# A two-layer decoder step on one core: three projections moved to the end of local attention, norms as background steps, an odd layer that begins on two chunks

## The chip, the core and the metric

The kernel runs on one core of a Trainium2 chip. The core has a matrix engine (TensorE, PE in the profile), VectorE (DVE), ScalarE (ACT), GpSimd (POOL) and a queue processor (SyncE, SP) that issues most DMAs; ScalarE issues the others. Each engine works through its own list of instructions in order and waits for the others by semaphores. The metric is the device time of one launch in microseconds (us).

## The reference

One inference step of a decoder trunk with two layers, for a prompt of 1024 tokens and 8 sample tokens with cached state. All is float32. Cut to what the change touches:

```python
for layer in range(2):
    h = rms_norm(x, norm_pre[layer])                  # x: 1024 + 8 tokens, 1024 channels
    mkv = memory_kv(mem, mem_norm[layer], w_mem_kv[layer])      # 256 memory tokens
    if layer == 0:   # even: gated delta rule | local attention | memory attention
        parts = [dilated_group(q[g], k[g], v[g], window, dil)   # 3 groups x 4 heads
                 for g, (window, dil) in enumerate(((128, 1), (512, 4), (2048, 16)))]
        o_b = combine_dilations(parts) * silu(gate_b)  # merged by softmax denominators
        o_m = memory_attend(q_m, mkv) * silu(gate_m)   # 4 heads of 128
        mix = concat(o_a * silu(z_a), o_b, o_m)        # 12 blocks of 128 channels
    else:            # odd: RG-LRU (8 blocks) | memory attention (4 heads)
        mix = concat(rg_lru(conv(xb)) * silu(gate), o_m * silu(gate_m))
    x = x + rms_norm(mix @ w_out[layer], norm_post[layer])
```

## The kernel before

Channels lie on the 128 partitions, tokens along the free axis, in three chunks of 352, 336 and 344 tokens (0, 1 and 2; the 8 sample tokens end chunk 2). A projection (`proj`) loads one 128-column block of weights as eight 128x128 tiles and makes, for each chunk, 24 matmuls: each tile is split into a rounded part and its remainder (`load_w`: ScalarE rounds, GpSimd or, for the output weights, VectorE subtracts), the activations likewise, and three of the four products are added in PSUM (`mm3`). So a projection is 72 matmuls.

The program is written in this order, and a scheduler then lays each engine's list; what has high priority goes first, the rest about as written.

1. Memory keys and values, the first norm, and the gated delta rule (`even_gdn`). In its last part four heads run one after the other in a chain of eight small steps each (`chain`: matmuls that go to VectorE and back, at L897, L900, L905 and L907). Projections are put beside it as cover: memory heads 0 to 2, and 11 results that are needed later and are parked in DRAM (`swa_ahead`, the dictionary `ahead`).
2. Local attention (`even_swa`): 36 query, key and value projections (4 heads x 3 window groups x 3), five of them parked ones. Beside them run two lanes of background work: `group` (scores, softmax, products of one head and group) and `combine` (the three groups of a head merged by factors that go through DRAM and come back broadcast, `sfb`). A lane is a generator; `tick`, called after each chunk of a projection, lets each lane do its next piece.
3. Output layer (`out_layer`): 8 output blocks x 12 mix blocks; first chunks 0 and 1 (mix blocks held in SBUF as `mah` and `mal`), then chunk 2. The norms (`chain_a`, `chain_b`, made of `tok_rstd` and `chan_rstd`: columns of sums on PE (`c`), an inverse root of twelve small VectorE steps (`x`, `y`, `t`), a diagonal `d` and a matmul `b` that spreads it) turn the result into the next layer's input `h1`. Tiles of the norm after the output are named `po0` and the chunk, of the next layer's pre-norm `pr` and the chunk.
4. The memory keys and values of layer 1 (`mem_kv(1)`, weights `mk1`, `mv1`), then the odd layer (`odd`: `query` makes `wq1`, `conv` makes `wx`), then its own output layer.

At the end of stage 2, before the change, memory head 3's query and gate come back from DRAM, all lanes are drained, memory head 3 attends (`ms`, `mt`, `mo`), and only then the combine of local head 3 starts (`slt` is its first matmul). The blocks of the mix are used in the order 0 to 3, 8 to 10, 4, 5, 6, 11, 7: memory head 3 is block 11, local head 3 is block 7.

## Time and profile before

| | us |
|---|---|
| median of 3 runs | 1944.48 (1942.31 to 1946.13) |
| the profiled execution | 1943.99 |
| its span, first to last instruction | 1942.2 |
| PE busy | 1789.0 (92%) |
| VectorE busy | 1081.1 (56%) |
| ScalarE busy | 716.3 (37%) |
| GpSimd busy | 540.2 (28%) |

The granted clock of PE is 0.949 of full speed on average. A busy share says how long an engine had work in it; matmuls are pipelined, so a busy PE at a low granted clock, or one with gaps just under the length of a record, may do half the work of a full one. "Idle before <- X" is the time an engine stood still before an instruction, and what ended it.

### The profile page before, as it was taken

The numbers are of one execution on the slowest core, as the hardware profiler recorded it, in microseconds if no ns is written. First come the engines' busy times: TensorE is split into PE (matmuls) and PEld (weight loads), VectorE is DVE, ScalarE is ACT, GpSimd is POOL, SyncE is SP. The second block draws the span as 40 slices with busy tenths as digits, with TensorE's granted clock in tenths as the row PEclk, the third lists the DMA queues.
The fourth block names the chain that finished last, engine by engine and source line by source line (L and its number), as shares of the span: only waits on it lengthen the run. The fifth ranks groups of instructions, "written<-read, shape, count | busy, mean of one in ns | idle before, by whom it ended". The sixth has DMA issues, their size and how long they took to land.

```text
span 1942.2 us, 29187 instructions
## 1 busy us (share of the span) xinstructions
PE 1789.0 (92%) x11341; PEld 1729.4 (89%) x11341; DVE 1081.1 (56%) x2302; ACT 716.3 (37%) x1610; POOL 540.2 (28%) x367
## 2 busy tenths in 40 slices
PE   6999999898999899999999976977899999989996
PEld 6799988798999899999999856967799999988996
DVE  7878759446633313525325556558655747667555
ACT  5355533123222243433333432324333434436432
POOL 3422224222211113232533202123532424330201
PEclk9999998898999999999999987978899999999998
DMA  8436455633425534645655424356733332223453
GB/s 288 177 130 217 153 173 190 213 114 116 177 102 197 188 120 148 239 143 180 221 184 193 140 67 151 114 154 223 257 133 143 130 111 96 78 71 125 144 193 135
DMA packets 160986, 307.30 MB, mean 158 GB/s; under 512 B 25104, under 2 KB 120528, under 8 KB 158928
## 3 DMA queue, kind: packets, MB, share of 16 engines
q1 hardware_dynamic: 67168, 222.99, 33.1%
q10 hardware_dynamic: 93680, 82.45, 13.0%
q8 instruction: 89, 1.46, 0.3%
q14 instruction: 49, 0.40, 0.1%
HBM read 254.58 MB, written 138.81 MB: 203 GB/s over the span
## 4 chain that ended last, share of the span: by engine, by line
PE 73%; DVE 15%; DMA 5%; ACT 3%; issue 2%; ACTq 1%; POOL 1%; SPq 0%; DVEq 0%; POOLq 0%
PE ss L992 1%; PE so L1025 1%; PE mo L373 1%; DVE tm L734 1%; PE ms L352 1%; PE gz L857 1%; PE gt L862 1%; DMA mf<-mixd 1%; PE st L1015 1%; PE mt L370 1%; DVE lacc L1270 1%; DVE got L934 1%; DVE xi L736 1%; DMA o_memv<-vf 1%; PE svp L977 1%
## 5 line engine op out<-in xcount | busy, mean ns | idle before, releaser
L994 DVE CUSTOM_DVE_ANT_0 spr<-ss,cs 128x128 f32<-128x128 f32 (+1 forms) x96 | 31.9, 348 | 84.9 <-PE ss L992 84.5
L1001 ACT ACTIVATE spr<-spr,snm 128x128 f32<-128x128 f32 (+1 forms) x96 | 42.2, 441 | 40.0 <-DVE snm L996 39.8
L628 DVE SCALAR_TENSOR_TENSOR acc<-pre,vec,acc 128x1024 f32<-128x1024 f32 x36 | 49.2, 1366 | 13.4 <-ACT acc L626 13.2
L1369 DVE TENSOR_TENSOR ya<-ya,ysq 128x352 f32<-128x352 f32 (+2 forms) x42 | 27.0, 645 | 37.4 <-ACT ysq L1368 37.4
L992 PE MATMUL ss<-sw,sw 128*128 128x128 f32 (+1 forms) x192 | 43.5, 330 | 4.1 <-DVE sml L994 2.8
L358 ACT ACTIVATE pm<-ms,nm 128x256 f32<-128x256 f32 x64 | 29.7, 472 | 47.0 <-DVE nm L356 34.7
L1427 POOL TENSOR_TENSOR y<-y,xr 128x352 f32<-128x352 f32 (+2 forms) x24 | 22.4, 936 | 84.9 <-DVE y L1426 84.3
L1384 POOL COPY mg<-mixs 128x8 f32<-128x8 f32 x24 | 7.7, 319 | 125.9 <-DVE wo01al L154 25.2
L372 DVE COPY mpt<-mt 128x512 f32<-128x512 f32 x32 | 22.0, 688 | 36.4 <-PE mt L370 36.3
L373 PE MATMUL mo<-mpt,vt 128*128 128x512 f32 x64 | 34.9, 628 | 4.9 <-DVE gnr L120 3.2
L978 DVE COPY svt<-svp 128x512 f32<-128x512 f32 x24 | 15.5, 684 | 41.6 <-PE svp L977 36.1
L1025 PE MATMUL so<-spt,svt 128*128 128x128 f32 x280 | 38.3, 275 | 0.2 <-ACT spt L1019 0.2
L1228 DVE SCALAR_TENSOR_TENSOR lacc<-lpre,vec,lacc 128x1024 f32<-128x1024 f32 x24 | 37.4, 1560 | 0.2
L1025 PEld LDWEIGHTS so<-spt,svt 128*128 128x128 f32 x280 | 36.3, 191 | 0.5 <-ACT spt L1019 0.5
L992 PEld LDWEIGHTS ss<-sw,sw 128*128 128x128 f32 x192 | 31.6, 195 | 5.3 <-DVE sml L994 3.3
L1225 DVE TENSOR_SCALAR lacc<-lpre,vec 128x1024 f32<-128x1024 f32 x8 | 19.4, 2419 | 23.7 <-ACT lpre L1220 23.7
L734 DVE TENSOR_TENSOR tm<-bl,xi 128x1 f32<-128x1 f32 (+30 forms) x31 | 28.5, 920 | 2.5 <-DMA bl<-aqd 2.0
L898 DVE TENSOR_TENSOR guu<-guu,gsc 128x128 f32<-128x128 f32 x28 | 8.0, 284 | 38.5 <-PE gsc L897 38.4
L162 PE MATMUL wo00p<-mah,wo00ah 128*128 128x352 f32 (+1 forms) x24 | 8.6, 401 | 22.5 <-ACT mah L1334 22.5
L370 PEld LDWEIGHTS mt<-cs,pm 128*128 128x128 f32 x128 | 17.5, 147 | 13.2 <-issue 8.0
L1019 ACT COPY spt<-st 128x384 f32<-128x384 f32 (+2 forms) x48 | 22.5, 475 | 17.4 <-PE st L1015 15.4
L352 PE MATMUL ms<-kt,qm 128*128 128x256 f32 x112 | 28.7, 387 | 0.0
(2149 smaller groups left out, 7344.4 us busy)
## 6 DMA issues: line engine op xcount, KB each, us to landing
o_sw3s<-cache_swa SPq DMA_DIRECT2D x64, 1023.5 KB
o_sw2s<-cache_swa SPq DMA_DIRECT2D x16, 1022.0 KB
gaq<-aqd ACTq DMA_DIRECT2D x20, 512.0 KB
mf<-mixd SPq DMA_DIRECT2D x19, 344.0 KB
sfb<-fd SPq DMA_DIRECT2D x12, 512.0 KB
aqd<-aq ACTq DMA_DIRECT2D x4, 1024.0 KB
o_sw3p<-sw SPq DMA_DIRECT2D x8, 512.0 KB
mixd<-lgt ACTq DMA_DIRECT2D x8, 512.0 KB
```

Source lines behind the costliest of these rows:

```text
L352: T.matmul(ps[:, b * 256:(b + 1) * 256], q[:, (b0 + b) * P:(b0 + b + 1) * P], kt[:, h, :], start=True, stop=True)
L358: S.activation(pr[:, b2 * 2 + b, :], ps[:, b * 256:(b + 1) * 256], AF.Exp, bias=nm[:, b0 + b:b0 + b + 1], scale=SC, accum_out=lt[:, b0 + b ...
L370: T.transpose(pt[:, b * P:(b + 1) * P], pr[:, b, kb * P:(kb + 1) * P], ident)
L373: T.matmul(po, vt[:, kb, h, :], st, start=kb == 0, stop=kb == 1)
L628: V.scalar_tensor_tensor(acc, pre[:, j:j + 1024], vc("gconv", ti * 4 + j), acc, ALU.mult, ALU.add)
L734: V.tensor_tensor(t3, bl[:, 0:i, i][:, None, :].broadcast_to([P, i, i]), xi[:, 0:i, 0:i].rearrange("p j c -> p c j"), ALU.mult)
L992: T.matmul(po, q[:, bb * P:(bb + 1) * P], k[:, k0:k0 + w], start=True, stop=True)
L994: V.tensor_tensor_reduce(pr[:, bb, :w], po, mask, 1.0, NEG, ALU.add, ALU.max, accum_out=ml[:, 0, g, bb:bb + 1])
L1001: S.activation(pr[:, bb, :w], pr[:, bb, :w], AF.Exp, bias=nm[:, bb:bb + 1], scale=SC, accum_out=ml[:, 1, g, bb:bb + 1])
L1025: T.matmul(po[:, (bb % 4) * P:(bb % 4 + 1) * P], vt[:, kb, :], pt[:, o:o + P], start=st, stop=sp_)
L1228: V.scalar_tensor_tensor(acc[:, :1024], pre[:, j:j + 1024], vc("lconv", ti * 4 + j), acc[:, :1024], ALU.mult, ALU.add)
L1369: V.tensor_tensor(acc[:, :n], acc[:, :n], sq[:, :n], ALU.add)
```

## The change

Local attention. The parked results are now 10. Memory head 3's query and gate and local head 3's gate are no longer among them, and two projections of local head 1, group 0 (query and key) are new. The three left out are projected in `even_swa` itself, after the last value projection and before the lanes are drained. The combine of head 3 is started by its lane like the others, memory head 3's attention calls `tick` four times, and the mix order ends with 7, 11.

Output layer. `tok_rstd` and `chan_rstd` become generators that give way after the squares and after the diagonal. In layer 0 the norms of chunks 0, 1 and 2 are lanes; before, they were issued at high priority. In layer 1 the norms are taken as lanes too for chunks 0 and 1.

Odd layer. The first query and the first convolution input are projected for chunks 0 and 1 first, then both for chunk 2. Their tiles move to a pool of their own, opened earlier. Two pools shrink to make room: `hf` from three buffers to two, `ysq` of layer 0 from two to one.

```diff
@@ even_gdn
-                    for key in ((), (), (("q3",), ("g3",), (1,)), ((0, 0, 1), (0, 0, 2), (2,), (3,)))[h]:
+                    for key in ((), (), ((1,), (2,), (1, 0, 0)), ((0, 0, 1), (0, 0, 2), (1, 0, 1)))[h]:
@@ mem_attend
+                if ticks:
+                    tick()
@@ even_swa
-                    if g == 2 and h < 3:
-                        lanes["group"].append([then("combine", combine(h, ml, nums, lambda acc, h=h: put(h, acc))), 0])
+                    if g == 2:
+                        done = (lambda acc, h=h: put(h, acc)) if h < 3 else (lambda acc: last.update(acc=acc))
+                        if h == 3:
+                            gt = sp.tile([P, 1024], F32, name="sg3", tag="sg")
+                        job = combine(h, ml, nums, done, gt if h == 3 else None)
+                        lanes["group"].append([then("combine", job), 0])
...
+            swa_gate(3, x, sp, gt)
+            qm = sp.tile([P, 1024], F32, name="qm03", tag="qkv", bufs=5)
+            mem_query(0, 3, x, I["we"][59], qm)
+            gm = mem_gate(sp, 0, 3, x, I["we"][63], "qkv", 5)
             sh0.close()
...
-            drain_lanes("cached", "group", "combine")
-            mem_attend(sp, 0, 3, qm, gm, gm, tags=("spr", "spt"))
-            mix_put(xa, order[-2], gm)
-            start("combine", combine(3, ml, nums, lambda acc: last.update(acc=acc)))
+            drain_lanes("cached", "group")
+            mem_attend(sp, 0, 3, qm, gm, gm, tags=("spr", "spt"), ticks=True)
...
@@ out_layer
-                    with tc.high_priority(offset=HP):
-                        if l:
-                            chain(m, xr[m])
-                        elif m == 0:
-                            chain_a(0, xr[0])
-                        else:
-                            chain_a(1, xr[1])
-                            chain_b(0)
-                            chain_b(1)
+                    start(f"norm{m}", chain(m, xr[m]))
...
-            with tc.high_priority(offset=HP):
-                chain(2, xr[2])
+            drain_lanes("norm0", "norm1")
             if l == 0:
+                start("norm2", chain(2, xr[2]))
+                tick()
                 mem_kv(1, mem_reload(pb), np_)
+                drain_lanes("norm2")
@@ odd
-                if n < 3:
+                if n == 0:
+                    q0 = query(0, (0, 1))
+                    begun = {0: conv_in(0, 0, (0, 1))}
+                    q0()
+                elif n < 3:
                     query(n)
-                conv(n, 0)
+                conv(n, 0, begun.get(0))
```

The first place in the order is PE's list at the end of local attention. `ws322p` is the last value projection, `wb3p`, `wq03p` and `wg03p` are the gate of local head 3 and the query and gate of memory head 3, `svp`, `ss` belong to the last window group, `slt` begins the last combine, and `wo00p` is the first output block. Before:

```order
L164 MATMUL ws322p_10523<-h0h_140,ws322l_10455 128x344
L977 MATMUL svp_10588<-cs,sw_10452 128x128 x4
...
L992 MATMUL ss_10604<-sw_10305,sw_10168 128x128
L162 MATMUL wo00p_10887<-mah_10559,wo00ah_10761 128x352
...
L370 MATMUL mt_10748<-cs,pm_10719 128x128 x4
L373 MATMUL mo_10739<-mpt_10753,vt_279 128x512
L1032 MATMUL slt_10778<-cs,sml_9307 48x128
L162 MATMUL wo00p_10887<-mah_10581,wo00ah_10768 128x352
```

Now:

```order
L164 MATMUL ws322p_10234<-h0h_140,ws322l_10165 128x344
L162 MATMUL wb3p_10278<-h0h_94,wb3h_10272 128x352
...
L162 MATMUL wq03p_10432<-h0h_94,wq03h_10426 128x352
...
L162 MATMUL wg03p_10556<-h0h_94,wg03h_10550 128x352
...
L1044 MATMUL slt_10592<-cs,sml_9032 48x128
L162 MATMUL wg03p_10598<-h0h_110,wg03h_10550 128x336
...
L164 MATMUL wg03p_10634<-h0h_140,wg03l_10551 128x344
L366 MATMUL ms_10694<-kt_278,qm_10424 128x256 x2
L162 MATMUL wo00p_10883<-mah_10667,wo00ah_10794 128x352
...
L389 MATMUL mo_10775<-mpt_10781,vt_279 128x512
L162 MATMUL wo00p_10883<-mah_10681,wo00ah_10801 128x352
```

Three projections stand where the output blocks stood, and `slt` has moved from behind memory head 3's attention to the middle of the last of them.

The second place is VectorE's list there. `mal` is the remainder of a mix block, `nm` the row maxima of memory head 3, `smm` and `sf` the factors of the combine, `snum` its large products, `sg` and `gm` or `smg` the gates. Before:

```order
L374 TENSOR_TENSOR smg_10584<-mo_10739,smg_10584 128x512
L1335 TENSOR_TENSOR mal_10582<-smg_10584,mah_10581 128x688
L1052 TENSOR_TENSOR smm_10804<-al_10788 8x128
...
L1063 SCALAR_TENSOR_TENSOR sf_10805<-sf_10805,smm_10804 8x384
L1078 TENSOR_TENSOR snum_9929<-snum_9929,sfb_10827 128x1024
L1080 TENSOR_TENSOR snum_10339<-snum_10339,sfb_10829 128x256x4
...
L1087 TENSOR_TENSOR snum_9929<-snum_9929,sg_10825 128x1024
L1335 TENSOR_TENSOR mal_10574<-snum_9929,mah_10573 128x688
```

Now:

```order
L368 TENSOR_REDUCE nm_10691<-ms_10694 128x2
L1361 TENSOR_TENSOR mal_10668<-mf_10807,mah_10667 128x688
...
L1064 TENSOR_TENSOR smm_10701<-al_10626 8x128
...
L1075 SCALAR_TENSOR_TENSOR sf_10702<-sf_10702,smm_10701 8x384
L1361 TENSOR_TENSOR mal_10678<-mf_10844,mah_10677 128x688
...
L1091 TENSOR_TENSOR snum_9644<-snum_9644,sfb_10725 128x1024
L154 TENSOR_TENSOR wo01al_11002<-wo01af_11000,wo01ah_11001 128x768
...
L1100 TENSOR_TENSOR snum_9644<-snum_9644,sg_10270 128x1024
L1361 TENSOR_TENSOR mal_10682<-snum_9644,mah_10681 128x688
L390 TENSOR_TENSOR gm_10548<-mo_10775,gm_10548 128x512
L1361 TENSOR_TENSOR mal_10690<-gm_10548,mah_10689 128x688
```

The combine stood alone behind memory head 3's attention; now its steps alternate with that attention and with the mix blocks.

The third place is PE's list at the end of the last delta-rule chain, where `gsc` are the chain's steps, `ws011p` is the projection beside it and `gf` begins the finish. Before:

```order
L897 MATMUL gsc_5709<-gS_5701,gWT_5592 128x128
L163 MATMUL ws011p_6280<-h0l_135,ws011h_6222 128x344
...
L164 MATMUL ws011p_6280<-h0h_140,ws011l_6223 128x344
L900 MATMUL gsc_5709<-guu_5591,gkd_5626 128x128
L905 MATMUL gsc_5709<-guu_5591,gaq_5510 128x128
L907 MATMUL gsc_5709<-gS_5701,gaq_5511 128x128
L935 MATMUL gf_6309<-cs,got_5635 128x128 x4
```

Now:

```order
L164 MATMUL ws011p_6179<-h0h_140,ws011l_6122 128x344
L912 MATMUL gsc_5698<-guu_5591,gkd_5626 128x128
L917 MATMUL gsc_5698<-guu_5591,gaq_5510 128x128
L919 MATMUL gsc_5698<-gS_5690,gaq_5511 128x128
L909 MATMUL gsc_5709<-gS_5701,gWT_5592 128x128
L912 MATMUL gsc_5709<-guu_5591,gkd_5626 128x128
L917 MATMUL gsc_5709<-guu_5591,gaq_5510 128x128
L919 MATMUL gsc_5709<-gS_5701,gaq_5511 128x128
L947 MATMUL gf_6208<-cs,got_5635 128x128 x4
```

The chain now ends with three matmul pairs and no projection between them, where before the last half step had 11 matmuls of a projection in it.

## Rows read from the trace of the kernel before

**Rows 1.** Seven stretches: engines' busy time, PE clock, DMA share; first line names the columns.

```profile
core 0: us, PE busy (x) PEld busy (x) DVE busy (x) ACT busy (x) POOL busy (x), PEclk, DMA share, GB/s
...
652.00:1102.50 450.50, 446.89 (x2961) 441.13 (x2961) 168.53 (x412) 163.84 (x388) 136.04 (x75) 0.99 0.52 176
1102.50:1144.50 42.00, 36.31 (x206) 32.08 (x204) 27.06 (x56) 18.54 (x47) 3.92 (x4) 0.92 0.40 130
1144.50:1184.40 39.90, 13.23 (x40) 9.29 (x40) 21.52 (x32) 5.93 (x16) 0.36 (x2) 0.62 0.19 59
...
1263.00:1296.20 33.20, 19.57 (x76) 16.84 (x75) 14.08 (x32) 4.88 (x10) 8.64 (x5) 0.65 0.46 139
1296.20:1337.10 40.90, 40.47 (x265) 39.43 (x264) 35.24 (x87) 23.39 (x50) 8.31 (x9) 0.99 0.75 254
1337.10:1391.00 53.90, 35.46 (x218) 32.88 (x217) 46.93 (x74) 22.65 (x42) 35.00 (x22) 0.76 0.58 200
1391.00:1411.50 20.50, 19.25 (x102) 18.70 (x101) 9.35 (x28) 4.68 (x10) 6.21 (x5) 0.80 0.63 234
```

**Rows 2.** PE timeline: start, duration, operation, idle before and its releaser.

```profile
1102.35 0.32 PE L164 MATMUL ws322p<-h0h,ws322l 128*128 128x344 f32 x1
...
1154.15 0.42 PE L1032 MATMUL slt<-cs,sml 128*48 128x128 f32 x1
...
1180.69 0.94 PE L162 MATMUL wo00p<-mah,wo00ah 128*128 128x352 f32 x2 [20.95 <-ACT mah L1334]
...
1184.37 0.32 PE L162 MATMUL wo02p<-mah,wo02ah 128*128 128x352 f32 x1
...
1195.64 0.32 PE L162 MATMUL wo03p<-mah,wo03ah 128*128 128x352 f32 x1
```

**Rows 3.** VectorE by form, 1102.5 to 1184.4: count, busy us, mean ns, idle before.

```profile
L1335 DVE TENSOR_TENSOR mal<-mf,mah 128x688 fp32r<-128x688 f32 x10 | 8.6, 870 | 2.3 <-ACT mah L1334 2.3
...
L421 DVE TENSOR_REDUCE sc2op<-sc2v 128x128 f32<-128x1152 f32 x3 | 6.6, 2194 | 0.0
```

**Rows 4.** VectorE timeline, last combine.

```profile
1169.63 1.23 DVE L1078 TENSOR_TENSOR snum<-snum,sfb 128x1024 f32<-128x1024 f32 x1 [5.60 <-DMA sfb<-fd]
```

**Rows 5.** PE timeline, end of the last delta-rule chain.

```profile
643.46 0.39 PE L897 MATMUL gsc<-gS,gWT 128*128 128x128 f32 x2
...
645.42 0.38 PE L900 MATMUL gsc<-guu,gkd 128*128 128x128 f32 x2
646.25 0.49 PE L905 MATMUL gsc<-guu,gaq 128*128 128x128 f32 x2 [0.44 <-DVE gS L902]
...
652.01 1.97 PE L935 MATMUL gf<-cs,got 128*128 128x128 f32 x8 [5.04 <-DVE got L934]
```

**Rows 6.** PE timeline, the last window group's steps.

```profile
1103.49 1.09 PE L977 MATMUL svp<-cs,sw 128*128 128x128 f32 x8 [0.82 <-ACT sw L495]
...
1106.48 0.49 PE L992 MATMUL ss<-sw,sw 128*128 128x128 f32 x2 [1.35 <-DVE svt L978]
...
1110.12 0.79 PE L992 MATMUL ss<-sw,sw 128*128 128x128 f32 x2 [1.66 <-DVE sml L994]
...
1118.10 0.71 PE L992 MATMUL ss<-sw,sw 128*128 128x128 f32 x4 [1.12 <-DVE sml L994]
```

**Rows 7.** VectorE timeline, norm of chunk 1.

```profile
1347.35 2.35 DVE L118 TENSOR_TENSOR pr1t<-pr1y 128x3 f32<-128x3 f32 x1
...
1350.12 0.15 DVE L119 SCALAR_TENSOR_TENSOR pr1t<-pr1t,pr1x 128x3 f32<-128x3 f32 x1
```

**Rows 8.** GpSimd timeline, same moment.

```profile
1347.29 2.40 POOL L154 TENSOR_TENSOR mk12l<-mk12f,mk12h 128x1024 fp32r<-128x1024 f32 x1 [0.32 <-ACT mk12h L152]
```

**Rows 9.** PE timeline, norms and the odd layer's start.

```profile
1355.83 0.90 PE L193 MATMUL pr1b<-pr1d,cs 128*128 128x336 f32 x1 [6.30 <-DVE pr1d L192]
...
1404.37 0.74 PE L193 MATMUL pr2b<-pr2d,cs 128*128 128x344 f32 x2
...
1406.37 0.42 PE L162 MATMUL wq10p<-h1h,wq10h 128*128 128x344 f32 x1 [1.25 <-ACT h1h L212]
```

More of the change, by code (lines that the diff above doesn't have):

```diff
@@ L167, in proj, with run, at_once @@
         w = load_w(aps, name)
-        for ci in chunks:
-            c0 = CH[ci][0]
-            n = x[ci][0][0].shape[1]
-            ps = banks["p"].tile([P, 512], F32, name=f"{name}p{ci}", tag="pp")
-            mm3(ps[:, :n], w, x[ci], pace)
-            drain(ci, c0, n, ps[:, :n])
-            tick()
+        def run(chunks):
+            for ci in chunks:
+                c0 = CH[ci][0]
+                n = x[ci][0][0].shape[1]
+                ps = banks["p"].tile([P, 512], F32, name=f"{name}p{ci}", tag="pp")
+                mm3(ps[:, :n], w, x[ci], pace)
+                drain(ci, c0, n, ps[:, :n])
+                tick()
+        run(chunks)
+        return lambda: run([c for c in (0, 1, 2) if c not in chunks])
+    def at_once(steps):
+        while True:
+            try:
+                next(steps)
+            except StopIteration as e:
+                return e.value
     def tok_rstd(pool, sqs, n, scale, name, pt=None):
@@ L276, in mem_norm @@
         rs = pool.tile([P, 256], F32, name="mrs0")
-        V.tensor_copy(rs, chan_rstd(pool, [xm[:, k, :] for k in range(8)], 256, "mr"))
+        V.tensor_copy(rs, at_once(chan_rstd(pool, [xm[:, k, :] for k in range(8)], 256, "mr")))
         nc.scalar.dma_start(out=rsd, in_=rs)
@@ L340, in silu_drain, with mem_attend @@
         return f
-    def mem_attend(pool, l, h, q, gate, mix, tags=("pm", "mpt")):
+    def mem_attend(pool, l, h, q, gate, mix, tags=("pm", "mpt"), ticks=False):
         kt, vt = kts[l], vts[l]
@@ L1067, in combine @@
                 fbs = []
-                gt = sp.tile([P, 1024], F32, name=f"sg{h}", tag="sg")
-                nc.sync.dma_start(out=gt, in_=ahead[h,])
+                if gt is None:
+                    gt = sp.tile([P, 1024], F32, name=f"sg{h}", tag="sg")
+                    nc.sync.dma_start(out=gt, in_=ahead[h,])
                 for g in range(3):
@@ L1135, in even_swa @@
             drain_lanes("combine")
-            mix_put(xa, order[-1], last["acc"])
-            nc.scalar.dma_start(out=mixd[0][:, 7, CA:], in_=last["acc"][:, CA:])
+            for k, t in ((7, last["acc"]), (11, gm)):
+                mix_put(xa, k, t)
+                nc.scalar.dma_start(out=mixd[0][:, k, CA:], in_=t[:, CA:])
             return xa, w0
@@ L1220, in d, with conv @@
                     S.copy(pre[:, 3 + c0:3 + c0 + w], ps)
-                proj([I["wo"][ti]], x, f"wx{ti}", d)
+                return pre, proj([I["wo"][ti]], x, f"wx{ti}", d, chunks)
+            def conv(n, m, begun=None):
+                ti = n * 2 + m
+                pre, rest = begun or conv_in(n, m)
+                rest()
                 G.tensor_copy(cs4[:, 3, ti], pre[:, 1027:1035])
@@ L1512, in body @@
     order = [0, 1, 2, 3, 4, 5, 8, 9, 10, 11, 6, 7]
-    xa, w0 = odd(h1, sh1, sxa, order)
+    xa, w0 = odd(h1, sh1, eo, sxa, order)
     assert not bulk
```

64 lines of the change are left out of this document (28 added, 36 removed).

## The prediction

> **What bounds the kernel now.** I read the busy shares first: PE is busy for 1789.0 of the 1942.2 us of the span, and no other engine comes near. So a gain can only come from time in which PE stands still or runs slowly, and the windows by stage say where that is [rows 1]. In local attention up to its last value projection (652.0 to 1102.5) PE is busy for 446.89 of 450.5 us at a granted clock of 0.99; there is nothing to gain there, and its length is the number of its projections. Behind it, from the last `ws322p` at 1102.35 to the first `wo02p` at 1184.37 [rows 2], PE is busy for 36.31 + 13.23 = 49.5 of 81.9 us, at 0.92 and then 0.62. The timeline says why: PE waits 20.95 us for the mix block `mah` before it can go on with `wo00p` [rows 2], that is, for the last combine, of which VectorE and a DMA broadcast (a wait of 5.60 us) are the chain [rows 4]. The second weak stretch is the output layer: 1263.0 to 1296.2 at a clock of 0.65, and 1337.1 to 1391.0 with 35.46 of 53.9 us at 0.76 [rows 1]. The third is the end of the last delta-rule chain, where PE waits 5.04 us for `got` [rows 5].
>
> The unit of the sum is a projection. `wo02p` takes 72 matmuls of the same widths from 1184.37 to 1195.64 [rows 2], and the next block begins right behind it: 11.27 us, in a full stretch.
>
> **The change part by part.** The count of projections stays the same. One goes from the delta rule, two from the middle of local attention, and three come to its end.
>
> *Delta rule.* One projection fewer is -11.27 us if PE is the bound there. But the last chain then ends with one more bare half step: from L897 to L900 it is 645.42 - 643.46 = 1.96 us, from L900 to L905 0.83 us, together 2.79 [rows 5], of which PE's own two records fill about 0.7 that it had to do anyhow. So +2.1, and -9.2. Bounds: -11.3 (the bare steps cost nothing) and 0 (the chain with its waits was the bound, and the projection lay free beside it). I take a value near the first, since before the change the projection ran up to one step from the chain's end, with no wait listed before the matmul at 645.42 that follows it [rows 5], which is what a full PE looks like.
>
> *Local attention, middle.* Two projections fewer, loaded instead: -22.5 us. Their loads are 512 KB each like those of the parked blocks, at a DMA share of 0.52 [rows 1], and far ahead of their use; at nothing. 29 projections now cover the window groups' steps instead of 31. Uncovered, one group waits 1.35 + 1.66 + 1.12 = 4.1 us [rows 6] (the last group is what shows it). For eleven groups, with 2 in 31 of the cover gone, that is 11 x 4.1 x 2/31 = 2.9 us. So -19.6; bounds -22.5 and, if the cover breaks everywhere, rival D.
>
> *The tail, last `ws322p` to first `wo02p`.* Before 81.9 us [rows 2]. Now three projections, 33.8 us, stand first, with the last group's steps between them; those of its matmuls that are listed take 1.09 + 0.49 + 0.79 + 0.71 = 3.1 us [rows 6], and I put the group at 5.5. So 39.3 us to the end of `wg03p`. What is late then is VectorE. It has 27.06 + 21.52 = 48.6 us of work in the old tail [rows 1]. Of that the three reductions `sc2op` (6.6 us [rows 3]) and the group's own steps (5, an estimate by the same share) now lie under the projections; 37 us are left: 12 remainders `mal` at 0.87 us [rows 3], the factors and products of the combine, memory head 3's maxima and gates. PE has less to do there. The 5.60 us of the broadcast [rows 4] now lie beside memory head 3 and the `mal` steps, since `slt` starts inside the last projection; the 20.95 us go with it. I add 4 us for the first drain and for the last rows of matmuls, which follow the last `mal`: 39.3 + 41 = 80.3, or -1.6. Below, PE's own work bounds it: 36.31 x 0.92 + 13.23 x 0.62 = 41.6 us at full clock [rows 1], + 33.8 = 75.4, or -6.5. Above, if the broadcast's wait stays and mix loads come late behind weights on SP's queue (another 3): +8. So two thirds of the gain of 32 us are there because the tail takes in three projections and gets no longer.
>
> *Norms as background steps.* The squares, roots and applications are the same instructions. What moves is their place: in the second pass the weight subtractions now go ahead of the first norm, and the norms of chunks 0 and 1 are spread over ticks. VectorE is the bound of 1296.2 to 1391.0, with 35.24 of 40.9 and 46.93 of 53.9 us [rows 1], and gets the same work. Where PE ends its pass sooner, it waits longer for the norm: 6.30 us before `pr1b` are such a wait now [rows 9]. Nothing in this part touches the mix loads and weights behind the 0.65 stretch. One buffer fewer for the squares makes ScalarE wait for an addition on VectorE in the middle of PE's slack; at nothing, and up to +3 where PE is full.
>
> *Odd start.* Two projections, each on chunks 0 and 1, can now run before chunk 2 of `h1` is there. The wait this covers is 1.25 us before `wq10p` [rows 9], and in 1391.0 to 1411.5 PE is already busy for 19.25 of 20.5 us, at 0.80 [rows 1]: matmuls of chunks 0 and 1 already ran there early. I take -2 for this and the norms together. Bounds: -10, if a good part of the 18.4 idle us of 1337.1 to 1391.0 is filled, and +5, if VectorE is asked for both.
>
> Sum: -9.2 - 19.6 - 1.6 - 2 = -32.4. Against the profiled execution's own 1943.99 us that is 1911.6; its time is within 0.5 us of the median of 1944.48, so no correction.
>
> **A rule against the change.** VectorE's 128x3 multiplication in the norm of chunk 1 took 2.35 us, the next step of the same size 0.15 [rows 7]; the long one began 0.06 us after a GpSimd subtraction of 2.40 us [rows 8], and ended with it. The Trainium skill ("SBUF — State Buffer", section "SBUF: two separate sides") says that a VectorE operation with two inputs in SBUF and a GpSimd operation that reads SBUF share a pair of ports which the first of them locks for its whole length, so that the other waits. The trace agrees here, with the 2.35 us. By the rule every such step of a norm that is moved beside a subtraction loses as much, which puts the sum where rival B has it; by the forecast the number of such meetings stays as it is.
>
> **Rivals.**
> A, less is given back: the delta rule is bound by its chain (0 instead of -9.2), or the tail takes the upper end (+8 instead of -1.6). For it: PE waits of 0.44 and 5.04 us stand in the chain [rows 5], and VectorE's 12 `mal` can delay the combine's factors. Against: PE's busy share of the stage. Either gives 1921, both 1930.
> B, the norms lose to GpSimd: each step of a norm that now falls beside a weight subtraction takes about 2.2 us more (2.35 - 0.15 [rows 7]). GpSimd is busy for 35.0 of 53.9 us [rows 1], so it already happens; spread-out norms meet perhaps two to four more of them: +4.4 to +8.8, which makes 1916 to 1920.
> C, the norms really overlap: half or more of the 18.4 idle us of 1337.1 to 1391.0 go, since both chunks' chains stand side by side and the odd layer's first blocks fill the rest. For it: waits such as the 6.30 us [rows 9]. Against: VectorE's 46.93 of 53.9 us. It gives some 11 less: 1900.
> D, slower: the window groups lose their cover. The place is 652 to 1102.5: with fewer projections, each of the eleven groups meets the end of its projections with steps left and pays the waits that the last group pays. At 4.1 us [rows 6] that is +45, and the time 1957; it decides from 32.4/11 = 3 us a group on. For it: the steps wait on VectorE and ScalarE in turn. Against: those two are busy for only 168.53 and 163.84 of 450.5 us [rows 1], and PE's list keeps projections between the steps.
> E, the change does not bring the work together: the combine still ends last and alone, because its DMAs wait behind loads. Then the tail is 81.9 + 33.8 less the last group's 4.1 us of waits that are covered, 111.6 us or +29.7, and -9.2 - 19.6 - 2 + 29.7 = -1.1: 1943.
>
> **How the numbers follow.** Chances: forecast 0.46, A 0.20, B 0.10, C 0.14, D 0.06, E 0.04. The forecast's own range is 1904 to 1920, from the tail's -6.5 and half of its upper end. To hold 8 in 10 I reach down to C's upper half and up through B and A's single cases: 1897 to 1932; D, E and the far ends stay out. What a measurement of this kernel can tell from no change is 0.2%, some 4 us. Faster by more than that: forecast, A, B and C, less a little for two of their bad ends falling together, 0.89; within it, E, 0.04; slower, D and such ends, 0.07.
>
> **What would show it.** In the profile after, the first `gf` some 9 us earlier than 652.01; the stretch from it to the last `ws322p` about 20 us shorter than 450.5, PE still at 0.99; no wait of 20 us before a `wo00p`, `slt` inside `wg03p`, and VectorE nearly full from the end of `wg03p` to the first `wo02p`, that stretch about 41 us; the rest from there to the end shorter by 2. Waits of more than 3 us at the groups' steps would make it wrong on D's side; a stretch between pass b and `wq10p` shorter by 10 or more, on C's; VectorE steps of 128x3 at 2 us in greater number, on B's.

## The result and the profile after

| | before | after |
|---|---|---|
| median, us | 1941.45 (7 runs, 1937.88 to 1946.13) | 1924.46 (7 runs, 1922.29 to 1933.14) |
| ratio | | 0.9921, 95% interval 0.9899 to 0.9943 |
| the profiled execution, us | 1943.99 | 1922.29 |
| its span, us | 1942.2 | 1920.5 |
| PE busy, us | 1789.0 | 1787.9 |
| VectorE busy, us | 1081.1 | 1090.9 |

The change saves 0.8% (0.6 to 1.0), about 15 us (11 to 20) by the ratio and 17 by the medians. The two profiled executions stand 21.7 us apart in span: the one of before was somewhat over its median, the one of after under it. PE's work is the same to 1.1 us; what went is time in which PE had none. The ranking of stages below is made on the two profiles, each stage from the end of the mark above it to its own.

| stage, us | before | after | moved | forecast |
|---|---|---|---|---|
| start to the last head's `gf` | 652.01 | 641.57 | -10.4 | -9.2 |
| to the end of the last `ws322p` | 450.66 | 433.65 | -17.0 | -19.6 |
| to the first `wo02p` (the tail) | 81.70 | 85.79 | +4.1 | -1.6 |
| to the first `wo03p` | 11.27 | 15.12 | +3.9 | 0 |
| rest of the output layer's first pass | 63.44 | 63.27 | -0.2 | 0 |
| its second pass | 78.18 | 78.31 | +0.1 | } -2 |
| norms, memory keys, to the end of `wx1p` | 95.85 | 95.43 | -0.4 | } |
| all behind it | 509.1 | 507.4 | -1.7 | 0 |

The windows of the changed kernel that answer to [rows 1], columns as there:

```profile
641.50:1074.90 433.40, 425.79 (x2813) 419.20 (x2814) 171.63 (x403) 159.23 (x378) 137.77 (x73) 0.99 0.54 182
1074.90:1116.20 41.30, 41.30 (x281) 41.05 (x280) 20.65 (x43) 13.13 (x39) 8.67 (x4) 1.00 0.18 58
1116.20:1161.00 44.80, 37.01 (x185) 30.03 (x183) 37.05 (x61) 17.60 (x39) 2.54 (x5) 0.92 0.43 141
...
1239.40:1276.70 37.30, 23.04 (x108) 20.84 (x108) 14.76 (x28) 7.47 (x15) 8.64 (x5) 0.76 0.54 162
1276.70:1317.70 41.00, 39.64 (x234) 37.82 (x232) 32.73 (x86) 19.74 (x41) 7.46 (x8) 0.92 0.57 190
1317.70:1371.50 53.80, 37.41 (x231) 35.47 (x230) 48.61 (x79) 22.36 (x41) 36.94 (x22) 0.81 0.71 245
```

The three projections (1074.9 to 1116.2) run at full clock with no gap, 41.30 of 41.3 us. Behind them VectorE is busy for 37.05 of 44.8 us, where the prediction had worked out 37 in 41; that is 83%, not the nearly full VectorE that it named as its sign. In the middle PE is idle for 7.6 us where before it was for 3.6 [rows 1]. The stretch of the low clock (0.65 before, 0.76 now) is still there, with 23.04 of 37.3, and so is that of the norms (37.41 of 53.8).

PE's timeline of after at the places of [rows 2, 5, 9] (start, duration, operation, idle before and what ended it):

```profile
634.68 0.39 PE L909 MATMUL gsc<-gS,gWT 128*128 128x128 f32 x2
635.55 0.49 PE L912 MATMUL gsc<-guu,gkd 128*128 128x128 f32 x2 [0.48 <-DVE guu L910]
...
641.57 1.97 PE L947 MATMUL gf<-cs,got 128*128 128x128 f32 x8 [4.38 <-DVE got L946]
...
788.39 1.56 PE L1004 MATMUL ss<-sw,sw 128*128 128x256 f32 x6 [2.35 <-DVE sml L1006]
891.78 0.39 PE L442 MATMUL mc02po<-cs,mc02op 128*128 128x8 f32 x2 [1.42 <-DVE mc02op L437]
1034.41 0.87 PE L989 MATMUL svp<-cs,sw 128*128 128x128 f32 x6 [2.51 <-ACT sw L511]
...
1074.90 0.32 PE L164 MATMUL ws322p<-h0h,ws322l 128*128 128x344 f32 x1
1108.39 0.27 PE L1044 MATMUL slt<-cs,sml 128*48 128x128 f32 x1
...
1150.86 2.07 PE L389 MATMUL mo<-mpt,vt 128*128 128x512 f32 x2 [3.78 <-DVE mpt L388]
...
1161.01 0.43 PE L162 MATMUL wo02p<-mah,wo02ah 128*128 128x352 f32 x1 [0.25 <-ACT ya L1391]
...
1176.13 0.43 PE L162 MATMUL wo03p<-mah,wo03ah 128*128 128x352 f32 x1 [3.59 <-ACT wo03ah L152]
...
1342.97 0.83 PE L206 MATMUL pr1b<-pr1d,cs 128*128 128x336 f32 x2 [3.79 <-DVE pr1d L203]
```

The wait of 20.95 us is gone, and `slt` starts inside `wg03p`. New are a wait of 3.78 us inside memory head 3's attention, one of 3.59 us before `wo03p`, and three in the middle, of 2.35, 1.42 and 2.51 us, all for VectorE or for ScalarE behind it. The wait before `pr1b` is 3.79 us, not 6.30.

VectorE's timeline of after, last combine (with [rows 4]):

```profile
1119.20 0.38 DVE L1064 TENSOR_TENSOR smm<-al 8x128 f32<-8x128 f32 x1
...
1124.22 1.12 DVE L380 TENSOR_SCALAR pm<-pm,lt 128x256 f32<-128x256 f32 x4
...
1131.44 0.54 DVE L1075 SCALAR_TENSOR_TENSOR sf<-sf,smm 8x384 f32<-8x384 f32 x1
...
1139.20 1.23 DVE L1091 TENSOR_TENSOR snum<-snum,sfb 128x1024 f32<-128x1024 f32 x1 [2.50 <-DMA sfb<-fd]
...
1150.72 1.21 DVE L1100 TENSOR_TENSOR snum<-snum,sg 128x1024 f32<-128x1024 f32 x1
```

From the first factor to the last it takes 12.8 us now (1119.20 to 1131.98), and 5.6 before (1158.44 to 1164.03), because maxima, probabilities and `mal` steps stand between them. The broadcast wait shrank from 5.60 to 2.50 us, but from `slt` to `wo02p` it is 52.6 us and not 30.2 [rows 2].

The chain of work that ended last, followed back through the tail of the changed kernel, has these pieces among others (start, duration):

```profile
1118.64 2.92 DMA mf<-mixd
...
1126.35 2.87 DMA mf<-mixd
...
1132.00 3.46 DMA fd<-sf
...
1135.48 3.70 DMA sfb<-fd
...
1150.20 0.61 DVE mpt L388
...
1150.86 2.07 PE mo L389 x2
```

Four DMAs make 12.95 of its 44.8 us: two loads of mix blocks, whose remainders stand in VectorE's list between the factors, and the factors' way to DRAM and back as a broadcast. Then come the combine's large products on VectorE. At 1150.20 the chain leaves the combine: a copy for memory head 3 (`mpt`) stands behind those products, and what ends last is memory head 3's mix block.

### The profile page after: what moved, and what is told of

Its sections match the earlier page's. It is cut to its first block, busy times and chain, and to the rows that moved or that the text cites. A ratio compares the mean times of both kernels' runs of the same rounds, so it can differ in the third digit from the quotient of the medians.

```text
span 1920.5 us, 29152 instructions
## 1 busy us (share of the span) xinstructions
PE 1787.9 (93%) x11341; PEld 1729.0 (90%) x11341; DVE 1090.9 (57%) x2302; ACT 715.8 (37%) x1610; POOL 550.3 (29%) x367
## 4 chain that ended last, share of the span: by engine, by line
PE 70%; DVE 14%; DMA 6%; ACT 3%; issue 3%; POOL 1%; ACTq 0%; SPq 0%; DVEq 0%; POOLq 0%
PE ss L1004 2%; PE so L1037 1%; DVE tm L746 1%; PE mo L389 1%; PE gz L869 1%; DVE y L1449 1%; PE ms L366 1%; PE gt L874 1%; PE st L1027 1%; DMA sc3k<-cache_swa 1%; DMA mf<-mixd 1%; DVE lacc L1291 1%; DMA sfb<-fd 1%; DMA gst<-state_gdn 1%; DVE xi L748 1%
## 5 line engine op out<-in xcount | busy, mean ns | idle before, releaser
L1006 DVE CUSTOM_DVE_ANT_0 spr<-ss,cs 128x128 f32<-128x128 f32 (+1 forms) x96 | 32.4, 349 | 89.4 <-PE ss L1004 89.2
L1450 POOL TENSOR_TENSOR y<-y,xr 128x352 f32<-128x352 f32 (+2 forms) x24 | 23.0, 963 | 98.2 <-DVE y L1449 97.7
L366 PE MATMUL ms<-kt,qm 128*128 128x256 f32 x128 | 32.8, 387 | 0.0
L366 PEld LDWEIGHTS ms<-kt,qm 128*128 128x128 f32 x128 | 23.8, 195 | 5.9 <-issue 2.2
L1031 ACT COPY spt<-st 128x384 f32<-128x384 f32 (+2 forms) x48 | 22.4, 477 | 15.3 <-PE st L1027 15.1
```

What stands on the lines that cost most here:

```text
L366: T.matmul(ps[:, b * 256:(b + 1) * 256], q[:, (b0 + b) * P:(b0 + b + 1) * P], kt[:, h, :], start=True, stop=True)
L1006: V.tensor_tensor_reduce(pr[:, bb, :w], po, mask, 1.0, NEG, ALU.add, ALU.max, accum_out=ml[:, 0, g, bb:bb + 1])
L1450: (V if k % 2 else G).tensor_tensor(yk[k], yk[k], xr[k], ALU.add)
```

## The experiments

Each is timed against the kernel before on the same chip. Stage times are those of one profiled execution each, in us:

| | ratio (95%) | median | to `gf` | middle | tail | to `wo03p` | first pass, rest | second pass | norms |
|---|---|---|---|---|---|---|---|---|---|
| changed kernel | 0.9921 (0.9899 to 0.9943) | 1924.5 | 641.6 | 433.7 | 85.8 | 15.1 | 63.3 | 78.3 | 95.4 |
| e1 local part alone | 0.9902 (0.9885 to 0.9919) | 1925.5 | 645.2 | 440.3 | 85.9 | 15.0 | 65.8 | 76.7 | 98.1 |
| e2 norms, odd start alone | 0.9984 (0.9970 to 0.9998) | 1938.3 | 655.4 | 449.9 | 80.1 | 11.3 | 59.5 | 79.1 | 95.9 |
| e3 sample rows early | 0.9848 (0.9831 to 0.9865) | 1912.6 | 645.2 | 436.6 | 111.0 | 13.7 | 57.8 | 52.9 | 91.4 |
| e4 one more in delta rule | 0.9883 (0.9866 to 0.9899) | 1919.3 | 652.2 | 430.8 | 86.1 | 11.4 | 62.0 | 75.9 | 95.2 |
| e5 gate last | 0.9947 (0.9928 to 0.9967) | 1930.0 | 643.4 | 436.9 | 90.8 | 9.8 | 68.6 | 78.8 | 95.0 |
| e6 two ticks | 0.9803 (0.9781 to 0.9826) | 1901.8 | 642.5 | 436.0 | 85.1 | 11.4 | 69.9 | 56.1 | 88.2 |
| e7 remainders on GpSimd | 0.9915 (0.9888 to 0.9942) | 1923.3 | 642.0 | 440.0 | 87.9 | 13.1 | 63.3 | 77.5 | 97.7 |
| e8 copies by SyncE | 0.9893 (0.9874 to 0.9911) | 1918.3 | 638.5 | 436.5 | 85.6 | 12.7 | 62.6 | 75.4 | 97.1 |
| e9 before, two ticks | 0.9883 (0.9864 to 0.9901) | 1917.6 | 655.4 | 449.7 | 81.8 | 11.6 | 72.1 | 59.6 | 81.1 |
| e10 e6 and e8 | 0.9772 (0.9750 to 0.9794) | 1893.9 | 644.2 | 430.8 | 86.2 | 11.4 | 69.2 | 53.6 | 91.3 |
| e11 combine spread | 0.9850 (0.9829 to 0.9872) | 1912.3 | 643.0 | 423.7 | 85.7 | 15.9 | 63.0 | 79.3 | 98.6 |
| e12 e10 and e11 | 0.9710 (0.9689 to 0.9731) | 1887.0 | 645.5 | 423.4 | 86.1 | 11.4 | 68.0 | 53.3 | 93.4 |

A column shows how far one execution can be trusted. The middle has the same code in the changed kernel, e1, e3, e5, e6 and e7, and takes 433.7 to 440.3, 437.2 on average; in before, e2 and e9 it takes 450.7, 449.9 and 449.7. So the two projections taken from it brought 12.9 us on average, and the -17.0 of the one profile is at the lucky end. "To `gf`" is 643.3 on average in the same six and 654.3 in the three: -11.0.

### Which part of the change brings it: e1 and e2

e1 takes from the change the delta rule, local attention and mix order, e2 the rest.

```diff
 e1: @@ out_layer, odd
-                    start(f"norm{m}", chain(m, xr[m]))     # and the rest of the norms and the odd start
+                    with tc.high_priority(offset=HP): ...  # as before
 e2: @@ even_gdn, even_swa, order
-                    for key in ((), (), ((1,), (2,), (1, 0, 0)), ((0, 0, 1), (0, 0, 2), (1, 0, 1)))[h]:
+                    for key in ((), (), (("q3",), ("g3",), (1,)), ((0, 0, 1), (0, 0, 2), (2,), (3,)))[h]:
```

> The kernel before with only the part of the change in the delta rule and local attention (10 parked results, three projections at the end, the last combine as a lane, the mix order); norms and odd layer as before. Theory 1 (by the traces of before and after: delta rule -10.4, middle -17.0, tail +4.1, first pass +3.7, all behind it -2): the whole gain is here, so about 20 us under before, within 3 us of the changed kernel. Theory 2 (the norms as background steps carry a part of the gain or of the loss that the two traces hide in each other): it differs from the changed kernel by over 4 us, to either side.

> The kernel before with only the norms as background steps and the odd layer that begins on two chunks; delta rule and local attention as before. Theory 1: nothing, 0 with 3 us to either side, VectorE gets the same work and is the bound of that stretch. Rival C of the prediction: the norms really overlap, -8 or more. Rival B: they meet GpSimd's subtractions, +4 to +9.

e1 gives 0.9902, 19 us (16 to 22), with the same tail, the same late `wo03p` and the same second pass as the changed kernel: theory 1. e2 gives 0.9984, 3 us (0 to 6): not nothing, but the forecast's -2, and neither C's 8 and more nor B's loss. The two parts alone make 22 us together, the whole change 15 (11 to 20): on top of e1 the norms and the odd start show no gain.

### The price of a projection: e4

```diff
@@ even_gdn
-... ((0, 0, 1), (0, 0, 2), (1, 0, 1)))[h]:
+... ((0, 0, 1), (0, 0, 2), (1, 0, 1), (1, 0, 2)))[h]:
```

> The changed kernel with one more projection beside the last delta-rule chain (the value projection of local head 1, group 0, parked and loaded), so 11 parked as before. Theory 1 (PE is the bound on both sides): the delta rule +9 to +10.5, the middle of local attention -8.5 to -11.3, together between -2 and +2. Rival A (the chain and its waits are the bound of the delta rule, the projection is free there): delta rule +0 to +3, together -6 to -11.

PE's timeline of e4, the last `gf`:

```profile
652.15 1.97 PE L947 MATMUL gf<-cs,got 128*128 128x128 f32 x8 [5.98 <-DVE got L946]
```

The projection costs the delta rule 652.15 - 643.3 = 8.9 us (10.6 against the changed kernel's own profile), so PE is the bound there and rival A's first half falls. In the middle it frees 437.2 - 430.8 = 6.4, and the change itself got 12.9 / 2 = 6.4 for each of its two. The 430.8 is one execution, of a stage that varies by 6.6 us: the size is uncertain. Together +2.5 by the stages; the whole came out at 0.9883, which is no loss but 7 us less than the changed kernel, of intervals that just touch. The other stages in which its profile is shorter (`wo03p` 3.7, second pass 2.4) have no edit in them; what part of the 7 us they are was not settled. A projection is worth 11.3 us in PE time and some 6.4 in the middle: that is the step to explain.

### Where the middle gave back: e11

What stands ahead of the three waits of the middle, in VectorE's, GpSimd's and ScalarE's timelines of the changed kernel:

```profile
784.83 3.29 DVE L1100 TENSOR_TENSOR snum<-snum,sg 128x1024 f32<-128x1024 f32 x1
...
885.83 4.04 DVE L1095 TENSOR_TENSOR snum<-snum,snum 128x1024 f32<-128x1024 f32 x1
```

```profile
784.64 2.40 POOL L409 TENSOR_TENSOR mc01k<-mc01k,mqb 128x1024 f32<-128x1024 f32 x1 [5.69 <-DMA mc01k<-cache_mem]
787.00 3.36 POOL L154 TENSOR_TENSOR ws200l<-ws200f,ws200h 128x1024 fp32r<-128x1024 f32 x1
```

```profile
1032.18 0.37 ACTq L1104 DMA_DIRECT2D mixd<-snum  x1
1032.65 1.05 ACT L152 CAST ws322h<-ws322f 128x1024 fp32r<-128x1024 f32 x1 [8.13 <-DVE snum L1100]
```

L1100 is the last of the six large steps of a combine (products and sums), L1095 its third. They stand in one piece ahead of the window group's or the sample lane's step for which PE waits at 788.39 and 891.78, and they are stretched: L1100 takes 3.29 us here and 1.21 at 1150.72, beside GpSimd products and subtractions of 2.40 and 3.36 us. At the third place ScalarE has to issue the store of the combine's result (`mixd<-snum`), which waits for an L1100. Behind that issue it stands for 8.13 us, with the drains of projections after it, and PE waits for the drains. With the projections as they stood before there is one such wait in the middle, of 2.65 us. In e1, with the same code as the changed kernel, the first of them is longer, as PE's timeline of e1 shows:

```profile
796.46 2.93 PE L990 MATMUL ss<-sw,sw 128*128 128x256 f32 x6 [6.26 <-DVE sml L992]
```

The stretch of `ws121p`, in which it falls, is 22.9 us there and 16.8 in the changed kernel. In e10, with the same 18 matmuls of a window group in it and a wait of only 0.24 us, it is 14.6.

Such a wait can also cost more than its length, by PE's clock. In the changed kernel matmuls of 336 columns start 0.15 us apart until 893.7, 1.9 us behind the wait that ended at 891.78, and 0.28 apart from there to 897.0. The windows of the changed kernel and of e1 there:

```profile
893.80:897.20 3.40, 3.40 (x14) 3.40 (x13) 3.31 (x3) 0.00 (x0) 0.00 (x0) 0.51 0.00 0
```

```profile
794.40:801.20 6.80, 4.74 (x14) 4.21 (x15) 4.08 (x17) 2.78 (x10) 0.71 (x1) 0.50 0.77 222
```

The granted clock is 0.5 in them (the lower of its two levels, 1.2 GHz) and 1.00 ahead of them. In the middle of the kernel before it is at that level for 6.5 us in all, in the changed kernel for 9.8, in e11 below for 3.3, where half of the time is lost. With PE's idle time that makes 3.6 + 3.3 = 6.9, 7.6 + 4.9 = 12.5 and 1.5 + 1.6 = 3.1 us, an estimate that accounts for the 5.5 us that the changed kernel's profile gave back of 22.5, and for what e11 gains.

```diff
@@ combine, for heads 0 to 2, ahead of four of the five large products after the first
+                        if gt0:
+                            yield 1
```

> The changed kernel; the combines of local heads 0 to 2 give way after each of their large VectorE products (four more steps each). Theory 1 (the middle of local attention gives back 6 to 9 us of its two projections because the six products of a combine, 10 to 13 us of VectorE in one piece, stand ahead of a window group's steps): the middle goes from 434 to 440 to 430 to 434, the whole -3 to -6. Theory 2 (what is given back are the group's own waits, spread over all groups): within 2 us of the changed kernel; or longer, if the next head's first group waits for the buffers that the combine holds longer.

The window of e11's middle:

```profile
643.00:1066.40 423.40, 421.93 (x2814) 416.30 (x2815) 167.13 (x402) 159.36 (x378) 136.15 (x73) 1.00 0.54 186
```

The middle takes 423.7 us, 13.5 under the average of the same code without it, and the whole is 0.9850, about 14 us under the changed kernel (intervals apart). PE is busy for 421.93 of 423.4 at a clock of 1.00. That is more than theory 1 asked: against the average before it is 26.4 us for two projections of 11.3, since before had a wait of that kind too. `ws121p` has no such wait now and takes 12.2 us, though with 6 matmuls of the group in it and not 18. The stage's loss was the combine's pieces, and not the groups' own waits, by which the prediction had priced it: e11 leaves one wait of over 0.7 us in the middle, of 0.88.

### The late `wo03p`: e8, and e3

ScalarE's timeline of the changed kernel, where the 3.59 us begin:

```profile
1173.85 0.45 ACT L1389 COPY y<-wo01p 128x352 f32<-128x352 f32 x1 [11.32 <-DMA sc3k<-sqd]
```

From 1162.5 on ScalarE has only DMA issues; the last of them are the copies of the sample rows from DRAM (`sc3k<-sqd`), which the row names as what ended the wait. The drains of `wo01p` and the rounding of `wo03p`'s weights stand behind them. But most of the wait had passed before the first copy, at 1171.20. The chain of work that ended last has a load of cached rows there, of 512 KB, and ScalarE's next issues (stores of sample rows) begin when it has landed:

```profile
1160.84 9.29 DMA sc3k<-cache_swa
```

```profile
1170.16 0.95 ACTq L1165 DMA_DIRECT2D o_sw3s<-sr3r  x2
```

In the kernel before, the row of the same drain, and the same load in the chain, are

```profile
1191.90 0.45 ACT L1363 COPY y<-wo01p 128x352 f32<-128x352 f32 x1 [6.68 <-PE wo02p L164]
```

```profile
1183.71 4.47 DMA sc3k<-cache_swa
```

so the same issues stood there with 6.68 us between two pieces of ScalarE's work, and `wo03p` still had its weights in time [rows 2]. The wait grew by 4.6 us and the load's time to land by 4.8. Why the load lands later is not shown.

```diff
@@ swa_cached
-                        nc.scalar.dma_start(out=t[0:P:16, 8, :], in_=scr[1 + c, g])
+                        nc.sync.dma_start(out=t[0:P:16, 8, :], in_=scr[1 + c, g])
```

> The changed kernel; the six small copies sc3k<-sqd and sc3v<-sqd of each head's sample rows are issued by SyncE and not by ScalarE. Theory 1 (ScalarE's list stood for 11.3 us behind such a copy in the first pass, and with it the weights of wo03p): the wait of 3.59 us before wo03p goes, from wo02p to wo03p it is 11.3 to 12 again, the whole -2 to -5. Theory 2 (SyncE's queue stands in its place, and the weights behind it come late): no gain or +2 to +5.

```profile
1173.20 0.43 PE L162 MATMUL wo03p<-mah,wo03ah 128*128 128x352 f32 x1 [1.16 <-ACT wo03ah L152]
```

In this PE row of e8 the wait is 1.16 us, and the stage takes 12.7 and not 15.1. ScalarE's row of e8 for the drain shows that the copies were the smaller part of its wait:

```profile
1171.27 0.45 ACT L1389 COPY y<-wo01p 128x352 f32<-128x352 f32 x1 [9.25 <-DMA o_sw3s<-sr3r]
```

The whole is 0.9893, some 5 us less than the changed kernel, with intervals that overlap slightly. The 2.1 us less on ScalarE are shown by the rows; the stage's 2.4 fit them, but e4 (11.4) and e11 (15.9) have the changed kernel's code in that stage and lie further apart. Where the rest of the 5 us comes from isn't shown.

```diff
@@ even_swa, main
-                             ((swa_cached, 1), (swa_cached, 2)), ())[h]:
+                             ((swa_cached, 1), (swa_cached, 2)), ((swa_cached, 3),))[h]:
-            drain_lanes("cached", "group")
+            drain_lanes("group")
-            drain_lanes("combine")
+            drain_lanes("combine", "cached")
-    late = [lambda ca: swa_cached(ca, 0, 3), lambda ca: mem_cached(ca, 0, 3)]
+    late = [lambda ca: mem_cached(ca, 0, 3)]
```

> The changed kernel; the cached attention of local head 3's sample tokens starts as a lane behind its last value projection and not in the output layer. Theory 1: ScalarE's queue no longer stands for 11 us in the first pass, so the wait of 3.59 us before wo03p goes; memory head 3's sample tokens, next in that lane, end sooner, so of the 14 us in which PE is idle between 1239.4 and 1276.7 most goes too: -4 to -16, about -12. Theory 2 (VectorE is the bound of the tail, and the three reductions of 2.2 us and their products on GpSimd that now fall into it cost as much as they save): 0 with 3 us to either side, and the stretch from the last wg03p to wo02p grows from 44.8 to over 50.

Both theories were half right. From `wo02p` on the two passes take 124.4 and not 156.7 us, and the tail grows from 85.8 to 111.0. PE's and ScalarE's timelines of e3 in the tail:

```profile
1137.47 0.45 PE L386 MATMUL mt<-cs,pm 128*128 128x128 f32 x1 [12.72 <-DVE pm L380]
```

```profile
1129.42 0.47 ACT L372 ACTIVATE pm<-ms,nm 128x256 f32<-128x256 f32 x1 [5.90 <-DMA sc3k<-cache_swa]
```

Issues of the same kind now hold ScalarE in the tail, with the landing of a load of cached rows named, ahead of memory head 3's exponentials, and PE waits 12.72 us behind them and VectorE. The sum is still 14 us better than the changed kernel.

### The idle second pass: e6 and e9

The sample rows of the last two heads go through a lane that moves one step at each tick, and a first pass has 16 ticks; what is left is drained at its end, where PE has nothing else. PE's longest wait of the changed kernel's second pass is for memory head 3's sample rows (`mc03`):

```profile
1267.14 0.59 PE L442 MATMUL mc03po<-cs,mc03op 128*128 128x8 f32 x2 [4.63 <-DVE mc03op L437]
```

```diff
@@ out_layer, one
                     tick()
+                    if l == 0 and tag == "a":
+                        tick()
```

> The changed kernel; in the first pass of the output layer tick is called twice after each chunk, so that the cached attention of the sample tokens ends in it. Theory 1 (the second pass stands because memory head 3's sample tokens end late): the second pass goes from 78 to 62 to 66 us, the first grows by 0 to 4, the whole -8 to -14. Theory 2 (the second pass stands for its weights and norms, not for the sample tokens): the second pass within 4 us of 78, the whole within 4 us.

> The kernel before, with nothing of the change; tick is called twice after each chunk of the output layer's first pass. Theory 1 (the idle time of the second pass was there before and the change left it): the second pass goes from 78 to 56 to 62, the first grows by 4 to 7, the norms behind shrink by up to 7, the whole -15 to -25, and with the change's own -17 to -20 this makes what the changed kernel with two ticks gained. Theory 2 (the second tick helps only where the norms are background steps or the sample rows come early): -8 or less.

Windows of e6: the first pass, the second, and to the end of `wx1p`:

```profile
1163.50:1244.80 81.30, 74.00 (x454) 72.28 (x455) 49.70 (x61) 25.73 (x57) 30.09 (x24) 0.96 0.56 172
1244.80:1300.90 56.10, 53.93 (x335) 52.18 (x333) 45.37 (x113) 28.27 (x58) 10.40 (x11) 0.97 0.63 205
1300.90:1389.00 88.10, 75.52 (x474) 73.78 (x475) 63.80 (x132) 33.69 (x65) 47.92 (x30) 0.86 0.63 224
```

The second pass is 56.1 us with PE busy for 53.93, in the changed kernel 78.3 with 62.68; the rest of the first is 6.6 longer, and `wo03p` comes in time. It is 23 us of the whole. That is more than theory 1 asked: the second pass fell further, and the norms behind are shorter too (88.2 and not 95.4). e9, the kernel before with the second tick alone, gives 0.9883, 22 us: the time was there before the change and has nothing to do with it, and the gains add up (0.9921 x 0.9883 = 0.9805, measured 0.9803). With this hold-up gone, the norms stage of e9 (81.1) is shorter than that of e6 (88.2), its second pass 3.5 longer: whether the norms as background steps cost some 4 us then is one profile's word, and was not tried by itself.

### What bounds the tail: e5 and e7

```diff
 e5: @@ even_swa
-            swa_gate(3, x, sp, gt)
             ...
             gm = mem_gate(sp, 0, 3, x, I["we"][63], "qkv", 5)
+            mem_attend(sp, 0, 3, qm, gm, gm, tags=("spr", "spt"), ticks=True)
+            swa_gate(3, x, sp, gt)
 e7: @@ mix_load
-        mix_put(xa, k, mf)
+        mix_put(xa, k, mf, G if l == 0 and k % 2 else V)
```

> The changed kernel; at the end of local attention memory head 3's query and gate are projected first, then it attends, and the gate of local head 3 is projected last. Theory 1 (the tail behind the last projection is bound by VectorE, with 37 of 44.8 us busy): the half of memory head 3's 9 us of VectorE work that moves under the last projection leaves it, the stretch from the last projection to wo02p goes from 44.9 to 38 to 41, the whole -4 to -7. Theory 2 (the stretch is bound by the combine's chain through DRAM): it stays at 44 to 46, and the whole within 2 us.

> The changed kernel; four of the ten remainders mal of the loaded mix blocks are made by GpSimd, which is busy for 2.5 of 44.8 us in the tail. Theory 1 (VectorE's work bounds the tail): 4 x 0.87 = 3.5 us less on VectorE, the tail 41 to 43, the whole -2 to -4. Theory 2 (GpSimd's subtraction shuts VectorE's out while it runs, as in rows 7 and 8): the four take as long there and VectorE's neighbours stretch, the tail 45 to 50, the whole 0 to +5.

Both speak against the reason that the prediction gave. In e5 VectorE has 33.8 us of work behind the last projection, 3 less, and the stretch takes 47.6 and not 44.9; the whole is 0.9947, no better and by its median 5.5 us worse, of intervals that overlap. Its products wait for the broadcast longer than in the changed kernel:

```profile
1153.15 1.22 DVE L1091 TENSOR_TENSOR snum<-snum,sfb 128x1024 f32<-128x1024 f32 x1 [4.65 <-DMA sfb<-fd]
```

In e7 four remainders (7.6 us on GpSimd) leave VectorE, and VectorE is busy for 38.1 us, 1 more than the changed kernel, since others stretch beside them. VectorE and GpSimd, with the four probability steps that took 1.12 us in the changed kernel:

```profile
1129.40 2.54 DVE L380 TENSOR_SCALAR pm<-pm,lt 128x256 f32<-128x256 f32 x4
```

```profile
1129.89 1.65 POOL L1361 TENSOR_TENSOR mal<-mf,mah 128x688 fp32r<-128x688 f32 x1 [3.01 <-ACT mah L1360]
```

The whole is unchanged (0.9915). One of the four probability steps took 1.75 us, the others 0.35: it began 0.05 us behind GpSimd's subtraction and ended 0.15 behind it. So a step taken from VectorE to GpSimd came back as 1.42 us of another's waiting. The lock of "SBUF — State Buffer" (the Trainium skill, section "SBUF: two separate sides") is said to hold not only for VectorE steps with two inputs but also for those in a two-port mode, which `tensor_scalar`, the operation of these steps, is said to be able to enter. The trace agrees that such a step can be held, with the 1.75 us; in which mode it ran the trace does not show.

So less work on VectorE did not shorten the tail. By the chain shown above it hangs on the combine, whose steps alternate with other work in VectorE's list and wait for DMAs, and then on memory head 3's attention behind it. That this chain is the bound is read from the rows; a kernel with the combine at high priority there was not run.

### All three: e10 and e12

> The changed kernel with two ticks in the first pass and with the small copies of sample rows issued by SyncE. If the two causes add up (-23 and -5 to -6): about 28 us under the changed kernel, 1895 to 1898. If the second tick already took what the copies cost (wo03p no longer waits in that run): 1900 to 1903, as with two ticks alone.

> The changed kernel with two ticks in the first pass, the small copies issued by SyncE, and the combines spread over more steps. The three act in different stages (second pass and first norm; first pass; middle of local attention), so by theory 1 they add up: -30 of the first two and -10 to -13 of the third under the changed kernel, 1881 to 1885. Rival: what the middle gains is given back, because the sample tokens' lanes end the later for it and meet the tail: 1890 to 1895.

e10 is 6 to 8 us under e6 (by ratio and by median; the intervals overlap slightly) and 30 under the changed kernel: the two add up in the whole. But `wo03p` comes in time in e6 already (11.4 us in both), so the sum does not come about by the cause that e8 was built on. The two profiles differ most in the middle (436.0 and 430.8), where the copies of the earlier heads move too; one execution each does not settle it. e12 gives 0.9710 (0.9689 to 0.9731), 1887.0 us, the best of the kernels here: 37 us under the changed one, near the 1881 to 1885 of the sum, and the middle takes 423.4 as in e11. The rival, 1890 to 1895, is out.

## Why the prediction was right in kind and too large

The direction and the mechanism were right: three projections fill the place where PE waited 20.95 us, and the delta rule and the middle get shorter. The size was too large: 17 us measured, 32.4 forecast, with 1924.5 outside the likeliest case's own range of 1904 to 1920 and inside the wide one. (The terms that the prediction names for that narrow range give about 1907 to 1917, and its 5.60 + 3 us above the tail's -1.6 give +7, not +8; neither changes the account.) Step by step:

- Delta rule, -9.2: measured -10.4 in the profile, -11.0 on average. Right, with e4 the other way round. The half step of the chain was overpriced: the 1.96 us were read where 11 matmuls of a projection stood in it [rows 5], and the bare half step takes 635.55 - 634.68 = 0.87 us.
- Middle, -19.6: this is a step that failed. It measured -12.9 on average (-17.0 in the one profile). The prediction priced the cover by the waits of one window group, 4.1 us, times a share [rows 6], 2.9 in all. What really comes is a few meetings with a combine's block of products, which lengthen the projection in which they fall by 2 and 8 us in the two cases shown (`ws121p`: 14.6 us without a wait, 16.8 and 22.9 with one), a part of it by the lower clock that follows. They hang on where the blocks lie, not on the share of cover; e11 takes them away and gets all of the 22.5 and 4 more.
- Tail, -1.6: measured +4.1, inside its bounds but for the wrong reason. The work on VectorE, 37 us, and the time to the end of `wg03p` (41 for 39.3) were well sized; the 4 us for waits were 7.7, and in e5 and e7 work taken from VectorE's list there didn't shorten it. "The 20.95 us go with it" is true; the stretch from `slt` to `wo02p` just takes 22 us longer.
- `wo03p`, 0: measured +3.9; over the five kernels with the changed kernel's code in that stage (it, e1, e4, e7, e11) it is 11.4 to 15.9 us, +2.8 on average. The prediction did not look at what ScalarE issues there. The issues stood there before as well; now they wait for a load that lands 4.8 us later, for a reason that stays open.
- Norms and odd start, -2: e2 measured -3 (0 to -6).

Rival B's extra price came once and not two to four times. Of the steps on 128x3 in the norms' stretch, four took 2.29 to 2.35 us in before and five, 1.98 to 2.31, in after, one of them:

```profile
1336.21 2.30 DVE L118 TENSOR_TENSOR pr1t<-pr1y 128x3 f32<-128x3 f32 x1
```

Rival C did not come either: the stretch stayed at 53.8 us. D and E are out by the stages; D had the right place and engine for the middle's waits, but they are a few and not one in each of eleven groups. A names nearly the size that was measured (1921). Its first place was wrong, the delta rule was not bound by its chain. Its second came in part: the tail took 5.7 of the 9.6 us, and the reason that A gives, `mal` steps that delay the combine's factors, is in the rows (12.8 us for 5.6).

## What to carry to other kernels

When work moves into an idle stretch, list everything that stands in that stretch and right behind it, on every queue, and ask where it goes; here it was a combine's chain and ScalarE's DMA issues. A block of large operations in one lane is paid by whoever stands behind it in the list, so let a lane give way between its large steps; here that was worth 14 us. And look for a lane that is drained at a stage's end: its ticks may simply be too few, which was worth more here (22 us, in either kernel) than the whole change.

## What the runs showed of the hardware

VectorE and GpSimd held each other up at sizes from 128x3 (2.3 for 0.15 us) to 128x1024 (3.29 for 1.21 us), also for a step with one tensor input, the probabilities scaled by a column (one of four steps took 1.75 us, the others 0.35). DMA issues on ScalarE that wait held all that stood behind them: for 11.32 us, most of it until a load had landed, and for 8.13 us until VectorE had made what was to be stored. Behind two of the three waits of the changed kernel's middle PE's granted clock fell to 0.5 for 3.4 us, so that a wait cost more than its length. And one and the same stretch of code, bound by PE, took 433.7 to 440.3 us in six profiles. Between the two ends the greater part is one wait, in `ws121p`, which went from 2.35 to 6.26 us and, with the lower clock beside it, stretched it by 6.1: a single profile does not size a stage of this kernel to better than some 5 us.
